# A fence behind the power of the attention output's norm, an earlier split of the FFN's first weights, and pair sums queued behind powers

## The chip, the cores and the metric

One core of one Trainium2 chip runs the whole program in one launch. The metric is the device time of one execution in microseconds. TensorE is called PE here, VectorE DVE, ScalarE ACT, GpSimd POOL; SyncE (SP) issues most loads.

## The reference

A trunk of two layers on 512 tokens of width 1024, all in float32. Layer 0 has multi-head latent attention, layer 1 attention over the frame's own chunk and 8 earlier ones, with a relative bias; both have a SwiGLU FFN of inner width 2816. Every part is wrapped in two norms.

```python
def rms_norm(x, g):
    xf = x.astype(jnp.float32)
    y = xf * lax.rsqrt(jnp.mean(xf * xf, axis=-1, keepdims=True) + EPS)
    return (y * g.astype(jnp.float32)).astype(x.dtype)

def swiglu(h, w_gate, w_up, w_down):
    return (jax.nn.silu(h @ w_gate) * (h @ w_up)) @ w_down

for layer in range(DEPTH):
    h = rms_norm(x, attn_pre_g[layer])
    y = mla_mixer(h, ...) if layer < N_A_LAYERS else chunked_mixer(h, ...)   # both end in o @ w_o
    x = x + rms_norm(y, attn_post_g[layer])
    h = rms_norm(x, ffn_pre_g[layer])
    f = swiglu(h, ffn_w_gate[layer], ffn_w_up[layer], ffn_w_down[layer])
    x = x + rms_norm(f, ffn_post_g[layer])
```

The change lies around `x + rms_norm(y, attn_post_g)` and the FFN's first products, and at the load of the first weights.

## The kernel before

**Layout.** Activations stand with the feature on the partitions: eight tiles of 128 features by 512 tokens. Every float32 product is made of three matmuls of rounded halves, hi by hi, lo by hi and hi by lo (`mm3`, L376 to L378). So each weight tile is split: a cast on ACT gives the high part (`whi`, L144), a subtraction on DVE the low part (`wlo`, L145).

**The feed.** A class `Feed` holds the plan of all weight tiles in the order in which they are used. `load` (L302) issues a load on SP into one of 5 raw buffers, `split` does the two halves into one of 3 hi and lo buffers of 1152 elements, or, with `room="h"`, into 512-wide pieces of another pool. `next` hands a split tile to the products, and `ahead(n)` loads and splits n tiles beyond it. `behind` names instructions behind which a split is to stand.

**Pairs and sums.** A part of the FFN's products is done in pairs with seven products in place of eight (`Pair`). Their weight sums are made by DVE (L183) and by accumulating transfers that POOL issues (`Pair.begin`, L170).

**The attention's output projection and its norm.** `out_proj` does most output tiles for all 512 tokens, and the last groups in two halves of 256 tokens, so that the norm of the first half runs beside the matmuls of the second. `Post.add_half` is that norm: the squares `sq` on ACT (L456), their sum `acc` on DVE (L462), two transposes `tot` on PE (L472), a reduction `ss` on DVE (L475), the power `r` = (mean + eps)^-0.5 on POOL (L480, in `rstd`), and two transposes on PE that spread `r` over the partitions (`bc`, L498). `apply` then multiplies `y` by `bc` (L668), adds x (L670) and makes the halves of the normalised x with which the FFN's products start. Behind the projection come the FFN's first weights: four chunks of `w_gu0`, then those of `w_gu`.

**The order.** The program is written out as it is to run, and a scheduler then orders each engine's instructions by priority: `first(n)` moves a piece n places earlier, and `tc.issue_after(ins)` makes an instruction stand behind another one, which acts only between instructions of the same engine. Each engine runs its row strictly in order.

Of the kernel before, what the change touches and what calls it, by code (L numbers as in the profile page):

```python
# [68 lines left out]
def trunk(ctx: ExitStack, tc: tile.TileContext, a, out):  # L69
# [73 lines left out]
    def split(dst_hi, dst_lo, src):  # L143
        return (nc.scalar.copy(dst_hi, src),  # L144
                V.tensor_tensor(dst_lo, src, dst_hi.bitcast(F32), op=OP.subtract))  # L145

    def split_scaled(dst_hi, dst_lo, src, col):
        return (nc.scalar.activation(dst_hi, src, AF.Copy, scale=col),
                V.scalar_tensor_tensor(dst_lo, src, col, dst_hi.bitcast(F32), op0=OP.mult, op1=OP.subtract))

    class Pair:
# [12 lines left out]
        def begin(self):  # L164

            r, self.made = self.raw, True
            r[0] = r[3] = r[6] = self.tile(2, wide[0], "sum", 2)
            r[4] = self.tile(2, wide[0], "sum2", 2)
            for j, n in ((0, 3), (4, 0)):
                nc.gpsimd.dma_start(r[j], self.src[n], accum_op=OP.add)  # L170

        def load(self, j):

# [89 lines left out]
    class Feed:  # L263


        def __init__(self):
            self.plan, self.raw, self.ready, self.pos, self.room = [], [], [], 0, {}
            self.behind, self.gate = {}, None

        def add(self, src, n, gain=None, room=None):  # L270
            self.plan.append((src, n, gain, room))
# [33 lines left out]
        def split(self, i):  # L305
            while len(self.ready) <= min(i, len(self.plan) - 1):
                j = len(self.ready)
                self.load(j + 2)
                raw, (src, n, gain, room) = self.raw[j], self.plan[j]
                for f in range(j, min(j + 8, len(self.plan))):  # L310
                    if f < j + 5 and isinstance(self.plan[f][0], Pair) or isinstance(self.plan[f][0], Down):
                        self.load(f)
                if isinstance(src, Down):
                    src.sums(*gain)
                    raw = src.at[gain]
                elif isinstance(src, Pair):
                    src.sums(gain)
                    raw = src.raw[gain]
                elif gain is not None and gain.shape[1] > 2:
                    rv = raw[:, :n].rearrange("p (a b) -> p a b", a=gain.shape[1])  # L320
                    with ExitStack() as st:
                        for b in self.behind.get(j, ()):
                            st.enter_context(tc.issue_after(b.ins))
                        V.tensor_tensor(rv, rv, gain, op=OP.mult)
                    gain = None
                if room is None:
                    at_ = 24 if isinstance(src, Pair) else 0
                    pieces = [tuple(wp.tile([P, 1152], F32R, tag=t, name=name_("w" + t), bufs=3)[:, at_:at_ + 1024]
                                    for t in ("hi", "lo"))]
                else:  # L330
                    pieces = self.room[room]()
                w = pieces[0][0].shape[1]
                if isinstance(raw, list):
                    c = 0
                    for t in raw:
                        c_ = slice(c, c + t.shape[1])
                        split(pieces[0][0][:, c_], pieces[0][1][:, c_], t)
                        c += t.shape[1]
                for c in range(0, 0 if isinstance(raw, list) else n, w):
                    m = min(w, n - c)  # L340
                    with ExitStack() as st:
                        for b in self.behind.get(j, ()):
                            st.enter_context(tc.issue_after(b.ins))
                        if gain is None or isinstance(src, Pair):
                            split(pieces[c // w][0][:, :m], pieces[c // w][1][:, :m], raw[:, c:c + m])
                            continue
                        for d in range(0, m, S):
                            split_scaled(pieces[c // w][0][:, d:d + S], pieces[c // w][1][:, d:d + S],
                                         raw[:, c + d:c + d + S], gain[:, (c + d) // S, 0:1])

                def at(c, m, pieces=pieces, w=w):
                    o = c % w
                    return tuple(t[:, o:o + m] for t in pieces[c // w])

                self.ready.append(at)
# [44 lines left out]
    def some(gen, n):  # L400

        last = None
        for _ in range(n):
            last = next(gen, None) or last
        return last
# [32 lines left out]
    class Sum:  # L438
# [28 lines left out]
        def total(self, h=None, ahead=0):  # L467
# [7 lines left out]
                V.reduce_sum(r, t[:, q[0] * P:(q[-1] + 1) * P].rearrange("p (a b) -> p a b", b=P), axis=AX.X)  # L475
            return r

    def rstd(v):
        r = small("r")[:, :v.shape[1]]
        nc.gpsimd.tensor_tensor(r, v, mhalf[:, :v.shape[1]], op=OP.pow)  # L480
        return r

    def rstd_of_scaled(ss, n, r0):
# [125 lines left out]
    class Post:  # L609
# [21 lines left out]
        def add_half(self, h, banks, rest, n1, n2, end=None):  # L631

            with first(40):
                ins = self.half(h, KT - len(banks), banks)
            if end:
                feed.behind[feed.pos] = feed.behind[feed.pos + 1] = ins
            with behind(end):
                at = some(rest, n1)
            with behind(end and at):
                v = self.sum.total(h, 200)  # L640
            with first(200):
                r = rstd(v)
            at = some(rest, n2)
            with behind(end and at):
                self.r[h] = spread(r, 2 * h)
# [37 lines left out]
    def out_proj(rhs, n_k, post, have, n_last, late):  # L683

        done = list(have)

        def weave(gen, each=4):
            ins = None
            for n, ins in enumerate(gen):
                if n % each == each - 1 and done:  # L690
                    post.add(done.pop(0))
            return ins

        groups = GROUPS[n_k][len(have) // 2:]
        for m in groups[:-n_last]:
            b = [bank() for _ in range(m)]
            weave(proj(m, n_k, KC[m], rhs, b))
            done.extend(b)
        last = groups[-n_last:]
        ws = {}  # L700

        def half(h, i, b):
            m, n, end = last[i], 0, i + 1 == n_last
            kc = KC[m]
            chunks = range(-(-n_k // kc))
            for c in chunks[::-1] if h and end else chunks:
                size = min(kc, n_k - c * kc)
                if not h:
                    ws[i, c] = feed.next(size * m * P, not end or c + 1 < len(chunks))
                for kk in range(size):  # L710
                    n += 1
                    for j in range(m):
                        yield mm3(b[j][:, HALF[h]], ws[i, c]((kk * m + j) * P, P), cut(rhs[c * kc + kk], HALF[h]),
                                  n == 1, n == n_k)
                if h and end and c >= len(chunks) - 2:
                    feed.ahead(len(chunks) - 1 - c)

        b = end = None
        for h in range(2):
            k = KT - sum(last)  # L720
            for i, m in enumerate(last):
                first_ = late and not h and not i
                before, b = b, [bank("s"), bank()] if first_ else [bank() for _ in range(m)]
                rest = half(h, i, b)
                if first_:
                    some(rest, 6)
                    for t in late:
                        run(t)
                if h and not i:
                    post.add_half(0, before, rest, 9, 11 if late else 8, end if late else None)  # L730
                elif i:
                    if not h:
                        some(rest, 2)
                    post.half(h, k - last[i - 1], before)
                end = weave(rest, 2 if first_ else 4)
                k += m
        return b

    class Split:
# [36 lines left out]

    def plan_ffn(i):
        for c in range(4):
            feed.add(a["w_gu0"][i, c], 1024, room="h" if c in (1, 2) else None)
        for f in range(N_WHOLE - 2):  # L780
            for c in range(2):
                feed.add(a["w_gu"][i, f, c], 1024)
        feed.add_pairs(a["w_pair"][i])
        feed.add_down(a["w_down"][i])
# [63 lines left out]
    for k in range(KT):  # L848
# [14 lines left out]
                mm3(b1[j], w(j * P, P), xs[k], False, k == KT - 1)  # L863
        if len(x) < KT:
            load_x()
        if k == 3:
            load_positions()
        if k:
            with ExitStack() as order:
# [644 lines left out]
    def products(xs, tb, rb, hid, aside=None):  # L1514
# [7 lines left out]
        for p in range(pairs):  # L1522
# [2 lines left out]
            gate = [U(name="gt") for _ in range(2)]  # L1525
            up_ = [U(name="ut") for _ in range(2)]
            for j in range(7):
                if aside is not None and p and j in (1, 3, 5):
                    next(aside, None)
                w = feed.next(1024, 2)  # L1530
                if p + 1 == pairs and j >= 4:
# [320 lines left out]
```

## Time and profile before

| | us |
|---|---|
| median of the runs | 1108.43 |
| lowest and highest of 3 runs | 1107.37, 1109.54 |
| profiled execution | 1108.42 |
| its span (first to last instruction) | 1106.5 |
| PE busy | 1092.9 |
| DVE busy | 908.8 |
| ACT busy | 679.0 |
| POOL busy | 118.2 |

The granted clock of PE was 0.998 of full speed over the span. The rows of the trace below give a start (us from the start of the span), a length, the engine, the line, the operation with its output and inputs, and in brackets how long the engine stood idle before it and what ended that. A row with x2 joins two instructions. A busy share near 100% says that an engine had work, not that every other engine was late: what PE waits for is read from the waits.

### The profile page before, as it was taken

To read this page: it belongs to the slowest core of one execution; us is meant where nothing else is said; L and a number is where in the kernel's file an instruction comes from. 1 tells how busy PE (TensorE), PEld (TensorE's weight loads), DVE (VectorE), ACT (ScalarE), POOL (GpSimd) and SP (SyncE) were. 2 spreads that over 40 slices of the span, in tenths; PEclk is the share of its full clock that TensorE was granted. 3 is DMA by queue.
4 is the path that set the end of the run, shared out by engine and by line. 5 is a ranking of instruction groups with operands and counts; after the bars stand their busy time and mean duration, and the time that the engine had idled before them with its cause. 6 is when DMAs were issued, how large, how long until landed. Compare 5 with 4: busy or idle time off the path is not lost. (4 is left out here: it accounts for less than half of the span.)

```text
span 1106.5 us, 19053 instructions
## 1 busy us (share of the span) xinstructions
PE 1092.9 (99%) x6893; PEld 978.6 (88%) x6893; DVE 908.8 (82%) x1651; ACT 679.0 (61%) x1319; POOL 118.2 (11%) x181
## 2 busy tenths in 40 slices
PE   9999999999999999999999999999999999999997
PEld 6887889999999998888888888889999999998885
DVE  7787747988878879978867888758988888889977
ACT  7575736755555556668635767656745555556675
POOL 2211100001000001500000110001000010002301
PEclk9999999999999999999999999999999999999999
DMA  7344227427677757961556677636438778859913
GB/s 239 117 118 138 66 69 256 153 76 193 171 205 182 178 171 247 160 193 47 190 146 169 166 193 189 162 115 215 162 92 214 207 198 220 210 177 280 172 29 76
DMA packets 88334, 181.47 MB, mean 164 GB/s; under 512 B 26816, under 2 KB 28608, under 8 KB 88240
## 3 DMA queue, kind: packets, MB, share of 16 engines
q1 hardware_dynamic: 74752, 147.10, 42.8%
q0 software_dynamic: 13056, 32.73, 16.7%
q8 instruction: 54, 0.88, 0.3%
q10 hardware_dynamic: 432, 0.44, 0.1%
q14 instruction: 40, 0.33, 0.1%
HBM read 148.88 MB, written 10.88 MB: 144 GB/s over the span
## 5 line engine op out<-in xcount | busy, mean ns | idle before, releaser
L144 ACT CAST whi<-raw 128x1024 fp32r<-128x1024 f32 (+3 forms) x224 | 225.4, 1006 | 218.2 <-PE al L1544 71.3
L145 DVE TENSOR_TENSOR wlo<-raw,whi 128x1024 fp32r<-128x1024 f32 (+3 forms) x224 | 261.0, 1165 | 62.9 <-ACT whi L144 61.9
L1544 PE MATMUL al<-th,whi 128*128 128x256 f32 x432 | 123.0, 285 | 0.2 <-ACT gt L1554 0.2
L1544 PE MATMUL al<-tl,whi 128*128 128x256 f32 x432 | 121.0, 280 | 0.0
L1544 PE MATMUL al<-th,wlo 128*128 128x256 f32 x432 | 121.0, 280 | 0.0
L376 PE MATMUL b<-xh,whi 128*128 128x512 f32 (+1 forms) x298 | 115.1, 386 | 0.0
L377 PE MATMUL b<-xl,whi 128*128 128x512 f32 (+1 forms) x298 | 109.9, 369 | 0.0
L378 PE MATMUL b<-xh,wlo 128*128 128x512 f32 (+1 forms) x298 | 109.5, 368 | 0.3 <-DVE wlo L145 0.3
L1544 PEld LDWEIGHTS al<-th,whi 128*128 128x128 f32 x432 | 81.3, 188 | 2.6 <-ACT gt L1554 0.4
L1544 PEld LDWEIGHTS al<-tl,whi 128*128 128x128 f32 x432 | 81.3, 188 | 0.0
L1544 PEld LDWEIGHTS al<-th,wlo 128*128 128x128 f32 x432 | 81.3, 188 | 0.0
L545 ACT ACTIVATE p<-p,mn 128x128 f32<-128x128 f32 (+1 forms) x96 | 54.1, 563 | 39.2 <-DVE mn L543 37.4
L145 DVE TENSOR_TENSOR ptl<-pt,pth 128x128 fp32r<-128x128 f32 (+1 forms) x96 | 46.6, 486 | 32.9 <-ACT pth L144 31.3
L145 DVE TENSOR_TENSOR wlo<-wd,whi 128x512 fp32r<-128x512 f32 x86 | 56.3, 685 | 14.6 <-ACT whi L144 14.4
L170 POOL DMA_DIRECT2D raw<-in_w_pair x32 | 28.0, 876 | 367.8 <-DMA raw<-in_w_pair 148.5
L378 PEld LDWEIGHTS b<-xh,wlo 128*128 128x128 f32 x298 | 56.2, 189 | 10.2 <-DVE wlo L145 0.7
L144 ACT CAST whi<-wd 128x512 fp32r<-128x512 f32 x86 | 49.8, 619 | 24.5 <-PE al L1300 10.7
L376 PEld LDWEIGHTS b<-xh,whi 128*128 128x128 f32 x298 | 56.5, 190 | 5.7 <-ACT whi L144 0.2
L377 PEld LDWEIGHTS b<-xl,whi 128*128 128x128 f32 x298 | 56.5, 190 | 5.5
L144 ACT CAST pth<-pt 128x128 fp32r<-128x128 f32 (+1 forms) x96 | 40.3, 422 | 30.3 <-PE pt L558 29.4
L1300 PE MATMUL al<-whi,pl 128*128 128x512 f32 x132 | 51.5, 390 | 0.0
L1300 PE MATMUL al<-whi,ph 128*128 128x512 f32 x132 | 51.4, 389 | 0.0
(319 smaller groups left out, 3301.0 us busy)
## 6 DMA issues: line engine op xcount, KB each, us to landing
raw<-in_w_pair SPq DMA_DIRECT2D x88, 512.0 KB, 4.4
raw<-in_w_pair POOLq DMA_DIRECT2D x32, 512.0 KB, 8.0
wd<-in_w_down SPq DMA_DIRECT2D x54, 256.0 KB, 6.0
raw<-in_w_o SPq DMA_DIRECT2D x16, 512.0 KB, 3.5
raw<-in_w_gu SPq DMA_DIRECT2D x16, 512.0 KB, 4.9
raw<-in_w_down SPq DMA_DIRECT2D x16, 512.0 KB, 4.2
raw<-in_w_qkb SPq DMA_DIRECT2D x16, 512.0 KB, 3.5
wd<-in_w_down POOLq DMA_DIRECT2D x22, 256.0 KB, 5.2
```

The lines of the kernel that those rows point to most:

```text
L144: return (nc.scalar.copy(dst_hi, src), V.tensor_tensor(dst_lo, src, dst_hi.bitcast(F32), op=OP.subtract))
L145: V.tensor_tensor(dst_lo, src, dst_hi.bitcast(F32), op=OP.subtract))
L170: nc.gpsimd.dma_start(r[j], self.src[n], accum_op=OP.add)
L376: nc.tensor.matmul(o, l[0], r[0], start=start, stop=False)
L377: nc.tensor.matmul(o, l[0], r[1], start=False, stop=False)
L378: last_mm[0] = nc.tensor.matmul(o, l[1], r[0], start=False, stop=stop)
L545: nc.scalar.activation(p[:, :n], p[:, :n], AF.Exp, bias=mn[:, :1], scale=-1.0, accum_out=self.sums[:, qt:qt + 1])
L1300: nc.tensor.matmul(to[e], l[c], r[d], start=j < 4 and k == 0 and n == 0, stop=k == NF // 2 - 1 and n == 2, skip_group_check=True)
L1544: nc.tensor.matmul(o, l[c], r[d], start=first_ and n == 0, stop=k == K2 - 1 and n == 2, skip_group_check=True)
```

## The change

Six edits:

1. In `add_half`, behind the power, DVE copies `r` into a small tile `f` (the fence). The next six splits of the feed are ordered behind this copy. This replaces an order that, in layer 1, held two splits behind the sums of the first half (`late`, and so `end`, is set in layer 1 only).
2. At the end of the first half in `out_proj`, `feed.ahead(3)` splits three tiles more, and all four chunks of `w_gu0` go to the 512-wide pieces.
3. The accumulating transfers of `Pair.begin` are ordered behind the last power issued.
4. `Feed.low` holds the last low part; a multiplication of weights by their gains (L324) is ordered behind it on DVE.
5. The positions are loaded at step 6 of the first projection, not at step 3.
6. A side job beside the FFN's pairs (`aside`) also advances at j = 0.

```diff
@@ Pair.begin
             for j, n in ((0, 3), (4, 0)):
-                nc.gpsimd.dma_start(r[j], self.src[n], accum_op=OP.add)
+                with tc.issue_after(last_pow[0].ins):
+                    nc.gpsimd.dma_start(r[j], self.src[n], accum_op=OP.add)
@@ Feed.split
-                        for b in self.behind.get(j, ()):
+                        for b in self.behind.get(j, ()) or (self.low,):
                             st.enter_context(tc.issue_after(b.ins))
                         V.tensor_tensor(rv, rv, gain, op=OP.mult)
...
-                            split(pieces[c // w][0][:, :m], pieces[c // w][1][:, :m], raw[:, c:c + m])
+                            self.low = split(pieces[c // w][0][:, :m], pieces[c // w][1][:, :m], raw[:, c:c + m])[1]
@@ rstd
+    last_pow = [None]
+
     def rstd(v):
         r = small("r")[:, :v.shape[1]]
-        nc.gpsimd.tensor_tensor(r, v, mhalf[:, :v.shape[1]], op=OP.pow)
+        last_pow[0] = nc.gpsimd.tensor_tensor(r, v, mhalf[:, :v.shape[1]], op=OP.pow)
         return r
@@ Post.add_half
             with first(40):
                 ins = self.half(h, KT - len(banks), banks)
-            if end:
-                feed.behind[feed.pos] = feed.behind[feed.pos + 1] = ins
             with behind(end):
                 at = some(rest, n1)
             with behind(end and at):
                 v = self.sum.total(h, 200)
             with first(200):
                 r = rstd(v)
+                fence = V.tensor_copy(small("f")[:, :v.shape[1]], r),
+            for n in range(len(feed.ready), len(feed.ready) + 6):
+                feed.behind[n] = fence
@@ out_proj
                 end = weave(rest, 2 if first_ else 4)
                 k += m
+            if not h:
+                feed.ahead(3)
@@ plan_ffn
         for c in range(4):
-            feed.add(a["w_gu0"][i, c], 1024, room="h" if c in (1, 2) else None)
+            feed.add(a["w_gu0"][i, c], 1024, room="h")
@@ first projection
-        if k == 3:
+        if k == 6:
             load_positions()
@@ FFN pairs
-                if aside is not None and p and j in (1, 3, 5):
+                if aside is not None and p and j in (0, 1, 3, 5):
                     next(aside, None)
```

How this moves instructions shows in each engine's row. In the names the number is a buffer's; `oh`, `ol` are the halves of the attention's output, `wh` those of the weights in 512-wide pieces, `whi` and `wlo` those in wide buffers, `b` a bank of products. All rows are of layer 1, around the end of the projection's first half.

DVE before, from the last sums ahead of the reduction of the first half:

```order
L462 TENSOR_TENSOR acc_1721_8676<-acc_1721_8676,sq_1746_8799 128x256
L462 TENSOR_TENSOR acc_1721_8676<-acc_1721_8676,sq_1747_8802 128x256
L145 TENSOR_TENSOR wlo_1760_8904<-raw_1722_8678,whi_1759_8903 128x1024
L145 TENSOR_TENSOR wlo_1798_9069<-raw_1761_8931,whi_1797_9068 128x1024
L475 TENSOR_REDUCE ss_1751_8839<-tot_1750_8836 128x2
L145 TENSOR_TENSOR wlo_1805_9108<-raw_1788_9025,whi_1804_9107 128x1024
L462 TENSOR_TENSOR acc_1721_8676<-acc_1721_8676,sq_1756_8869 128x256
L668 TENSOR_TENSOR y_1720_8674<-y_1720_8674,bc_1753_8864 128x256
```

DVE now, at the same place:

```order
L145 TENSOR_TENSOR wh_1767_8842<-raw_1755_8819,wh_1766_8841 128x512
L145 TENSOR_TENSOR wh_1769_8844<-raw_1755_8819,wh_1768_8843 128x512
L463 TENSOR_TENSOR acc_1727_8688<-acc_1727_8688,sq_1772_8851 128x256
L463 TENSOR_TENSOR acc_1727_8688<-acc_1727_8688,sq_1773_8854 128x256
L476 TENSOR_REDUCE ss_1777_8891<-tot_1776_8888 128x2
L463 TENSOR_TENSOR acc_1727_8688<-acc_1727_8688,sq_1783_8923 128x256
L644 COPY f_1779_8895<-r_1778_8893 128x2
L463 TENSOR_TENSOR acc_1727_8688<-acc_1727_8688,sq_1784_8926 128x256
L672 TENSOR_TENSOR y_1726_8686<-y_1726_8686,bc_1780_8918 128x256
```

Ahead of the reduction there now stand the sums, and behind it no `wlo` but the fence; eight 512-wide subtractions have come ahead of the sums.

ACT before, from the last group of squares of the first half to the first square of the second:

```order
L456 ACTIVATE sq_1746_8799<-b_1733_8727 128x256
L456 ACTIVATE sq_1747_8802<-b_1734_8728 128x256
L618 ACTIVATE y_1748_8805<-b_1733_8727,gains_70 128x256
L618 ACTIVATE y_1749_8807<-b_1734_8728,gains_70 128x256
L144 CAST whi_1759_8903<-raw_1722_8678 128x1024
L144 CAST whi_1797_9068<-raw_1761_8931 128x1024
L144 CAST whi_1804_9107<-raw_1788_9025 128x1024
L456 ACTIVATE sq_1756_8869<-b_1744_8797 128x256
```

ACT now, up to the same group's squares (`sq_1772`, `sq_1773`):

```order
L144 CAST wh_1751_8811<-raw_1728_8690 128x512
L144 CAST wh_1753_8813<-raw_1728_8690 128x512
L144 CAST wh_1756_8821<-raw_1741_8741 128x512
L144 CAST wh_1758_8823<-raw_1741_8741 128x512
L144 CAST wh_1761_8831<-raw_1750_8809 128x512
L144 CAST wh_1763_8833<-raw_1750_8809 128x512
L144 CAST wh_1766_8841<-raw_1755_8819 128x512
L144 CAST whi_1816_9131<-raw_1760_8829 128x1024
L144 CAST wh_1768_8843<-raw_1755_8819 128x512
L144 CAST whi_1868_9392<-raw_1765_8839 128x1024
L457 ACTIVATE sq_1772_8851<-b_1739_8739 128x256
L457 ACTIVATE sq_1773_8854<-b_1740_8740 128x256
```

Ten casts, two of them of 1024 elements and of chunks behind `w_gu0`, now stand ahead of the squares on which `acc` and `tot` rest.

PE now, from just ahead of `tot` to `bc` (before, 21 matmuls stood between the two, and `tot` stood 23 rows earlier):

```order
L378 MATMUL b_1781_8921<-ol_1600_8161,wh_1742_8743 128x256
L473 MATMUL tot_1776_8888<-ident_87,acc_1727_8688 128x128 x2
L379 MATMUL b_1781_8921<-oh_1599_8160,wh_1743_8744 128x256
L377 MATMUL b_1782_8922<-oh_1599_8160,wh_1742_8743 128x256
L378 MATMUL b_1782_8922<-ol_1600_8161,wh_1742_8743 128x256
L379 MATMUL b_1782_8922<-oh_1599_8160,wh_1743_8744 128x256
L377 MATMUL b_1781_8921<-oh_1649_8343,wh_1742_8743 128x256
L378 MATMUL b_1781_8921<-ol_1650_8344,wh_1742_8743 128x256
L501 MATMUL bc_1780_8918<-ident_87,r_1778_8893 128x128 x2
L379 MATMUL b_1781_8921<-oh_1649_8343,wh_1743_8744 128x256
```

Six matmuls are left between `tot` and `bc`; in layer 0 it is ten.

More of the change, by code (lines that the diff above doesn't have):

```diff
@@ L267, in __init__ @@
             self.plan, self.raw, self.ready, self.pos, self.room = [], [], [], 0, {}
-            self.behind, self.gate = {}, None
+            self.behind, self.gate, self.low = {}, None, None
         def add(self, src, n, gain=None, room=None):
@@ L344, in split @@
                         if gain is None or isinstance(src, Pair):
-                            split(pieces[c // w][0][:, :m], pieces[c // w][1][:, :m], raw[:, c:c + m])
+                            self.low = split(pieces[c // w][0][:, :m], pieces[c // w][1][:, :m], raw[:, c:c + m])[1]
                             continue
                         for d in range(0, m, S):
-                            split_scaled(pieces[c // w][0][:, d:d + S], pieces[c // w][1][:, d:d + S],
-                                         raw[:, c + d:c + d + S], gain[:, (c + d) // S, 0:1])
+                            self.low = split_scaled(pieces[c // w][0][:, d:d + S], pieces[c // w][1][:, d:d + S],
+                                                    raw[:, c + d:c + d + S], gain[:, (c + d) // S, 0:1])[1]
                 def at(c, m, pieces=pieces, w=w):
```

## The prediction, made before the changed kernel was run

> **What bounds the kernel now.** The page's busy table comes first: its columns are busy time, share of the span and instructions of each engine.
>
> ```profile
> PE 1092.9 (99%) x6893; PEld 978.6 (88%) x6893; DVE 908.8 (82%) x1651; ACT 679.0 (61%) x1319; POOL 118.2 (11%) x181
> ```
>
> TensorE (PE) is the bound: 1106.5 us of span less 1092.9 leaves 13.6 us in which it does nothing. None of the edits removes a matmul, so this change can only gain what PE waits for. The table of PE's waits (us in total, times, longest) says what that is:
>
> ```profile
> PE bc L498 <- POOL r L480: 1.9, 2, 1.4
> ...
> PE b L378 <- DVE wlo L145: 0.3, 1, 0.3
> ...
> ```
>
> The first row is the place of the change: twice, once in each layer, the broadcast `bc` of the norm's first half waits for the power on POOL. The last row shown is at the start. The rows left out are places that no edit touches. The timeline of PE around the two places (start, length, instruction, in brackets the idle time):
>
> ```profile
> 180.32 0.38 PE L472 MATMUL tot<-ident,acc 128*128 128x128 f32 x2
> ...
> 182.92 0.28 PE L378 MATMUL b<-oh,wh 128*128 128x256 f32 x1
> 183.79 0.43 PE L498 MATMUL bc<-ident,r 128*128 128x128 f32 x2 [0.58 <-POOL r L480]
> ...
> 756.45 0.38 PE L472 MATMUL tot<-ident,acc 128*128 128x128 f32 x2
> ...
> 759.06 0.28 PE L378 MATMUL b<-oh,wh 128*128 128x256 f32 x1
> 760.69 0.43 PE L498 MATMUL bc<-ident,r 128*128 128x128 f32 x2 [1.36 <-POOL r L480]
> ```
>
> From `tot` to the last matmul before `bc` go 2.60 us (182.92 - 180.32) for 2 transposes and 20 steps, 0.118 us a step. The start of `bc` is 0.87 and 1.63 us after the start before it; less one step that is 0.75 us lost in layer 0 and 1.51 in layer 1. DVE and POOL show why:
>
> ```profile
> 757.37 1.23 DVE L145 TENSOR_TENSOR wlo<-raw,whi 128x1024 fp32r<-128x1024 f32 x1 [0.65 <-ACT whi L144]
> 758.51 0.42 DVE L475 TENSOR_REDUCE ss<-tot 128x2 f32<-128x256 f32 x1
> 758.84 1.21 DVE L145 TENSOR_TENSOR wlo<-raw,whi 128x1024 fp32r<-128x1024 f32 x1
> ...
> 182.21 1.52 POOL L480 TENSOR_TENSOR r<-ss,mhalf 128x2 f32<-128x2 f32 x1 [12.96 <-DVE ss L475]
> 759.08 1.56 POOL L480 TENSOR_TENSOR r<-ss,mhalf 128x2 f32<-128x2 f32 x1 [12.16 <-DVE ss L475]
> 770.97 0.74 POOL L480 TENSOR_TENSOR r<-ss,mhalf 128x2 f32<-128x2 f32 x1 [10.33 <-DVE ss L475]
> ```
>
> `tot` is ready at 756.83, but the reduction starts at 758.51, behind a 1.23-us subtraction `wlo`; then the power takes 1.56 us beside the next `wlo` (758.84 to 760.05), where the same power alone took 0.74. In the second half (770.97) `bc` had 42 matmuls of cover and waits for nothing.
>
> **The fence and the early split.** Both keep `wlo` away from the reduction and the power. What the chain then needs, from the same rows and the second half's reduction:
>
> ```profile
> 770.41 0.42 DVE L475 TENSOR_REDUCE ss<-tot 128x2 f32<-128x256 f32 x1
> ```
>
> `tot` 0.38, a hand-over that I put at 0.1 (POOL to PE takes 0.06 at 183.73), reduction to power 0.56 (770.41 to 770.97), power 0.74, hand-over 0.06: 1.84 us. What covers it is shorter now: the order has 10 matmuls between `tot` and `bc` in layer 0 and 6 in layer 1, where it had 21. With the 2 transposes that is 12 and 8 steps, 1.42 and 0.94 us. So if `acc` is in time, 0.42 us are lost in layer 0 (gain 0.33) and 0.90 in layer 1 (gain 0.61). The wait does not go; it shrinks.
>
> Bounds for layer 0: with the power still at 1.52 the loss is 1.20 (gain -0.45); with no loss left, 0.75. I take 0.35, since the row without a subtraction, 770.97, is the one that the order now resembles: behind the reduction stands only the fence, in layer 1 an `acc` as well. The Trainium skill, "SBUF — State Buffer", in the section on who interferes with whom, says that a DVE operation with two SBUF inputs locks out a GpSimd one that reads SBUF. By that rule layer 1's `acc`, with two such inputs, still holds the power for some 0.3 us, and the sum below would be 0.6, the time 1107.8; this trace agrees on the direction with 1.52 and 1.56 against 0.74.
>
> **What now stands ahead of the squares.** The fence orders DVE alone. ACT's casts of the split are free to run, and the order puts eight half-wide casts of the first FFN weights and one (layer 0) or two (layer 1) 1024-wide casts of later chunks ahead of the last squares on ACT, on which `acc`, `tot`, the power and `bc` hang. The rows that price this:
>
> ```profile
> 174.21 0.90 ACT L618 ACTIVATE y<-b,gains 128x256 f32<-128x256 f32 x2
> ...
> 748.93 1.19 ACT L144 CAST wh<-raw 128x512 fp32r<-128x512 f32 x2
> 749.96 0.72 ACT L456 ACTIVATE sq<-b 128x256 f32<-128x256 f32 x2
> 750.49 0.91 ACT L618 ACTIVATE y<-b,gains 128x256 f32<-128x256 f32 x2
> 753.05 0.74 ACT L456 ACTIVATE sq<-b 128x256 f32<-128x256 f32 x2 [1.65 <-PE b L378]
> 756.29 1.05 ACT L144 CAST whi<-raw 128x1024 fp32r<-128x1024 f32 x1 [0.83 <-DMA raw<-in_w_gu]
> ...
> 753.47 0.96 DVE L462 TENSOR_TENSOR acc<-acc,sq 128x256 f32<-128x256 f32 x2 [1.58 <-ACT sq L456]
> ```
>
> Layer 1: the casts can start at 751.40 (750.49 + 0.91); two take 1.03 to the next start (748.93 to 749.96), so eight end at about 755.5, and two wide ones, 0.95 each (1.05 less the overlap with the next), at 757.4. From squares to the end of `acc` is 1.38 (753.05 to 754.43): 758.8. `tot` stands 23 steps later than before, at 756.45 + 23 x 0.118 = 759.16, so ACT's work alone is in time by 0.35 us. But the last cast also needs its load, the sixth of the gate and up weights, whose buffer comes free only when the first chunk is split: two casts to 752.4 and a subtraction of 512, half of 1.23, so about 753.1. The time of these loads from issue to landing has two rows (count, KB each, median us), around layer 1 and around layer 0, and the transfer that ran beside them one on the page:
>
> ```profile
> raw<-in_w_gu SPq DMA_DIRECT2D x7, 512.0 KB, 4.4
> ...
> raw<-in_w_gu SPq DMA_DIRECT2D x6, 512.0 KB, 7.5
> ...
> raw<-in_w_pair POOLq DMA_DIRECT2D x32, 512.0 KB, 8.0
> ...
> 745.98 0.94 POOL L170 DMA_DIRECT2D raw<-in_w_pair  x1 [39.42 <-DMA raw<-in_w_pair]
> ```
>
> With 4.4 it lands at 757.5; cast 0.95, squares and sums 1.38, so `tot` at 759.85 and `bc` at 761.7, against 759.16 + 0.94 = 760.1 without a wait: 1.6 lost, 0.1 more than before. With 3.7 or less it costs nothing and the gain is 0.61. The accumulating transfer that POOL started at 745.98 is gone from this stretch, which speaks for the shorter time, and 4.4 was measured beside it; I take a gain of 0.25, between -0.1 and 0.61, with -0.3 as the end for 4.6. Layer 0 by the same rows: casts from 175.1, eight to 179.2, one wide one to 180.2, `acc` at 181.5, against `tot` 11 steps later at 181.6: in time.
>
> **The pair sums behind the powers.** Two accumulating transfers a layer now queue on POOL behind the three powers, the last of which is the FFN's:
>
> ```profile
> 795.24 1.07 POOL L480 TENSOR_TENSOR r<-ss,mhalf 128x4 f32<-128x4 f32 x1 [22.67 <-DVE ss L475]
> ...
> 829.62 1.23 DVE L183 TENSOR_TENSOR raw<-raw,raw 128x1024 f32<-128x1024 f32 x1
> ```
>
> So they start at 796.3 instead of 745.98 and 771, and with the page's 8.0 us have landed by 806. The first pair sum that reads such a tile is at 829.62, with its split just ahead: some 20 us of cover. Cost 0; without the cover, 8 us a layer.
>
> **The start.** The positions' loads move behind three loads of `w_aq`:
>
> ```profile
> 15.13 1.35 SPq L837 DMA_DIRECT2D pos_i<-in_positions  x3
> 16.57 1.79 SPq L302 DMA_DIRECT2D raw<-in_w_aq  x4
> ...
> 20.94 0.84 ACT L144 CAST whi<-raw 128x768 fp32r<-128x768 f32 x1 [0.70 <-DMA raw<-in_w_aq]
> ...
> 21.91 0.41 PE L376 MATMUL b<-xh,whi 128*128 128x512 f32 x1
> 22.16 0.40 PE L377 MATMUL b<-xl,whi 128*128 128x512 f32 x1
> 22.82 0.50 PE L378 MATMUL b<-xh,wlo 128*128 128x512 f32 x1 [0.26 <-DVE wlo L145]
> ...
> 24.41 0.22 DVE L894 CAST rot<-pos_i 128x128 f32<-128x128 int32 x1
> ```
>
> `w_aq` is issued 1.4 us sooner. Its cast had waited 0.70 for the load, its `wlo` then held PE back: 0.66 us from start to start, where the step before was 0.25, so 0.41 us. That can go whole, or stay if the loads share the DMA with the others: 0 to 0.41. I take 0.3, since the cast's wait of 0.70 is shorter than the 1.4. The positions are read at 24.41; they now go out by about 18.4 (16.57 + 1.79), 6 us ahead, where `w_aq`, a far larger load, was cast 4.4 us after its first issue. In time: 0.
>
> **The gains behind the low parts, and the earlier side steps.** `low` only orders DVE's multiplications of weights by gains behind the previous split; `aside` advances one place earlier in a stage in which PE waits for nothing. Both have PE's queue of ready work as cover, and cost 0.
>
> **The second half.** The next six splits wait for the second fence too, so three `wlo` stand right behind it and ahead of the normalised x of that half. Each takes 1.2 us; PE has 42 matmuls, 5 us, there. I put 0 to 0.5 us of loss, and take 0.
>
> **The sum.** 0.35 + 0.25 + 0.3 = 0.9 us. The profiled execution took 1108.42 (span 1106.5 and 1.9 around it), the median of the runs is 1108.43, so both give 1107.5. From no change a measurement here can tell about 0.2%, 2.2 us (below 1106.2 or above 1110.6).
>
> **Rivals.** (a) *All three waits vanish.* 0.75 + 1.51 + 0.41 = 2.67, to 1105.7. For it: the reduction and power no longer meet a `wlo`. Against: 6 and 10 matmuls do not cover 1.84 us. A second way to the same time is the clock (two starts, and windows with the busy time of PE, PEld, DVE, ACT and POOL, the granted clock, the DMA share and GB/s):
>
> ```profile
> 104.65 0.48 PE L378 MATMUL b<-ckh,wlo 128*128 128x512 f32 x1
> 107.05 0.49 PE L1088 MATMUL sc<-kh,qh 128*128 128x128 f32 x2 [1.92 <-ACT kh L144]
> ...
> 108.00:111.40 3.40, 3.40 (x15) 3.25 (x14) 2.78 (x8) 1.15 (x5) 0.92 (x2) 0.50 0.98 306
> ...
> 750.00:775.00 25.00, 23.64 (x198) 23.43 (x197) 20.63 (x45) 16.50 (x39) 3.15 (x3) 1.00 0.64 192
> ```
>
> After PE's gap of 2.4 us the granted clock was 0.50 for 3.4 us (108.0 to 111.4), which costs 1.7 us; the gap of 1.5 us at 759 brought none (1.00 from 750 to 775). A start that is shifted by a few tenths may spare it: 1107.5 - 1.7 = 1105.8. The Trainium skill, "TensorE: Matmul & The Clock Gate", says of what happens there that utilisation is judged in free-running windows of 3413 ns and one idle window halves the clock; by that, whether this gap is hit depends on its phase, and the 3.4 us of the row agree with the length.
>
> (b) *ACT's queue holds the norm back; slower.* If the sixth load takes 7.5 us, it lands at 760.6, the squares start at 761.5, `tot` 762.9, `bc` 764.8 against 760.1: 4.7 lost where 1.51 were, 3.2 worse. A gap of that length would also bring the half clock, 1.7. Less 0.65 for the other terms: 4.25, to 1112.7. It decides from about 5.5 us on, where PE's gap (2.7) passes that of 104.65. For it: the 7.5 of layer 0; against: the transfer beside it then is gone.
>
> (c) *Nothing is gained.* `acc` doubles the power again and the second half's splits delay x by 0.5: in the terms' order -0.1, -0.1 and 0.3, less 0.5: 0.4 slower, 1108.8.
>
> **Chances.** The forecast 0.55 (1106.4 to 1108.5), (c) 0.12, (a) 0.19, (b) 0.14. Faster is (a), 0.19; slower is (b), 0.14; the same is the rest, 0.67. The range reaches to (a) at 1105.7, and above to a half clock window met by the forecast or a load a little past its median, 1107.5 + 2.3 = 1109.8; (b) is left out.
>
> **What would show it.** `bc` waits of about 0.4 and 0.7 to 1.7 us in PE's waits; powers of 0.74 to 1.1; no wait of L378 at 22; squares of layer 1 starting near 757.5 to 758.5, idle before them owed to a load; accumulating transfers near 218 and 795. Wrong it is if the squares start after 760, or if another matmul appears among PE's waits.

## The result

In 20 executions of each, the changed kernel took 1107.61 us in the median (1104.39 to 1109.72) and the kernel before 1111.95 (1107.37 to 1117.6). The ratio is 0.9961, with a 95% interval of 0.9947 to 0.9975: 4.3 us faster, of which the interval leaves 2.8 to 5.9. The three times of before that stood ahead of the prediction (1107.37, 1108.43, 1109.54) are the first of its 20 and lie among the fastest seven; the changed kernel's median is about as fast as the fastest of before, and none of its executions goes beyond 1110.

The two profiled executions show nothing of this gain: 1108.42 with a span of 1106.5 before, 1109.37 with a span of 1107.4 after. The busy table after:

```profile
PE 1094.4 (99%) x6893; PEld 979.9 (88%) x6893; DVE 909.3 (82%) x1659; ACT 680.5 (61%) x1323; POOL 117.1 (11%) x181
```

PE's waits after (us in total, times, longest):

```profile
PE sc L1094 <- ACT kh L144: 1.9, 1, 1.9
PE warm L113 <- DVE idle L110: 1.2, 1, 1.2
PE bc L501 <- POOL r L483: 0.9, 2, 0.7
PE b L377 <- ACT y L621: 0.8, 1, 0.8
PE al L1550 <- ACT gt L1560: 0.2, 1, 0.2
PE b L379 <- DVE wlo L145: 0.2, 1, 0.2
```

The wait of `bc` fell from 1.9 to 0.9 and did not go, and a matmul of layer 1 that had not waited now waits 0.8 for a bank. The timeline of layer 1 after, first ACT, then DVE, POOL and PE:

```profile
750.77 3.83 ACT L144 CAST wh<-raw 128x512 fp32r<-128x512 f32 x7
755.46 1.05 ACT L144 CAST whi<-raw 128x1024 fp32r<-128x1024 f32 x1 [0.86 <-DMA raw<-in_w_gu]
...
757.49 1.05 ACT L144 CAST whi<-raw 128x1024 fp32r<-128x1024 f32 x1 [0.46 <-DMA raw<-in_w_gu]
758.45 0.65 ACT L457 ACTIVATE sq<-b 128x256 f32<-128x256 f32 x2
758.99 0.84 ACT L621 ACTIVATE y<-b,gains 128x256 f32<-128x256 f32 x2
...
760.34 0.42 DVE L476 TENSOR_REDUCE ss<-tot 128x2 f32<-128x256 f32 x1 [0.53 <-PE tot L473]
760.68 0.42 DVE L463 TENSOR_TENSOR acc<-acc,sq 128x256 f32<-128x256 f32 x1
...
760.92 0.77 POOL L483 TENSOR_TENSOR r<-ss,mhalf 128x2 f32<-128x2 f32 x1 [54.04 <-DVE ss L476]
...
759.51 0.38 PE L377 MATMUL b<-oh,wh 128*128 128x256 f32 x1 [0.84 <-ACT y L621]
...
759.87 0.44 PE L473 MATMUL tot<-ident,acc 128*128 128x128 f32 x2
761.74 0.43 PE L501 MATMUL bc<-ident,r 128*128 128x128 f32 x2 [0.72 <-POOL r L483]
```

The reduction now follows `tot` at once, and the power takes 0.77 where it took 1.56. But ACT stands twice at casts for loads (0.86 and 0.46) before it comes to the squares at 758.45, and so `tot` starts at 759.87. The copy `y` (L621) behind the squares frees a bank, which is the new wait.

So the question is where 4.3 us come from, if one execution of each shows none of it.

### The profile page after: what moved, and what is told of

Read it like the earlier page. It is cut to its first block, busy times and chain, and to the rows that moved or that the text cites. A ratio compares the mean times of both kernels' runs of the same rounds, so it can differ in the third digit from the quotient of the medians.

```text
span 1107.4 us, 19059 instructions
## 1 busy us (share of the span) xinstructions
PE 1094.4 (99%) x6893; PEld 979.9 (88%) x6893; DVE 909.3 (82%) x1659; ACT 680.5 (61%) x1323; POOL 117.1 (11%) x181
## 5 line engine op out<-in xcount | busy, mean ns | idle before, releaser
L144 ACT CAST whi<-raw 128x1024 fp32r<-128x1024 f32 (+3 forms) x220 | 221.7, 1008 | 208.7 <-PE al L1550 69.4
L145 DVE TENSOR_TENSOR wlo<-raw,whi 128x1024 fp32r<-128x1024 f32 (+3 forms) x220 | 256.5, 1167 | 69.4 <-ACT whi L144 68.3
L377 PE MATMUL b<-xh,whi 128*128 128x512 f32 x234 | 96.7, 414 | 0.0
L379 PE MATMUL b<-xh,wlo 128*128 128x512 f32 x234 | 91.9, 393 | 0.2 <-DVE wlo L145 0.2
L378 PE MATMUL b<-xl,whi 128*128 128x512 f32 x234 | 91.7, 392 | 0.0
L379 PEld LDWEIGHTS b<-xh,wlo 128*128 128x128 f32 x234 | 43.9, 188 | 10.5 <-DVE wlo L145 0.9
L1306 PE MATMUL al<-wlo,ph 128*128 128x512 f32 x132 | 51.3, 389 | 0.0
L184 DVE TENSOR_TENSOR raw<-raw,raw 128x1024 f32<-128x1024 f32 x40 | 48.9, 1223 | 0.5
```

The lines of the kernel that those rows point to most:

```text
L144: return (nc.scalar.copy(dst_hi, src), V.tensor_tensor(dst_lo, src, dst_hi.bitcast(F32), op=OP.subtract))
L184: V.tensor_tensor(t, x, y, op=OP.add)
L377: nc.tensor.matmul(o, l[0], r[0], start=start, stop=False)
L378: nc.tensor.matmul(o, l[0], r[1], start=False, stop=False)
L379: last_mm[0] = nc.tensor.matmul(o, l[1], r[0], start=False, stop=stop)
L1306: nc.tensor.matmul(to[e], l[c], r[d], start=j < 4 and k == 0 and n == 0, stop=k == NF // 2 - 1 and n == 2, skip_group_check=True)
```

## The experiments

Each kernel was timed in turn with the kernel before on the same chip, in three batches; ratios are against before. The microseconds gained or lost in the text are the ratio's share of before's time; the differences of the medians (before: 1110.61 beside e1 to e4, 1111.35 beside e5 to e8, 1110.79 beside e9 to e12) lie up to about 1 us from them. "Sums" is edit 3, "low" edit 4, "positions" edit 5, "aside" edit 6, as they are numbered in the change.

| kernel | median us | ratio, 95% interval | executions |
|---|---|---|---|
| before, unchanged (e1) | 1110.68 | 1.0009 [0.9993, 1.0024] | 12 |
| before + sums (e2) | 1108.08 | 0.9968 [0.9955, 0.9982] | 12 |
| before + fence + early split (e3) | 1114.60 | 1.0032 [1.0017, 1.0046] | 11 |
| before + low + positions + aside (e4) | 1107.79 | 0.9969 [0.9956, 0.9981] | 11 |
| before + low (e5) | 1109.27 | 0.9981 [0.9969, 0.9992] | 12 |
| before + aside (e6) | 1109.82 | 0.9991 [0.9978, 1.0004] | 12 |
| before + positions (e7) | 1109.70 | 0.9988 [0.9974, 1.0002] | 12 |
| changed, without fence and early split (e8) | 1105.09 | 0.9951 [0.9932, 0.9970] | 6 |
| changed (e9) | 1107.31 | 0.9965 [0.9951, 0.9979] | 12 |
| changed, without early split (e10) | 1104.81 | 0.9943 [0.9926, 0.9960] | 6 |
| changed, without fence (e11) | 1107.16 | 0.9963 [0.9950, 0.9976] | 8 |
| e8 again (e12) | 1104.71 | 0.9941 [0.9925, 0.9957] | 6 |

**e1, the kernel before once more.** No edit.

> The kernel before, unchanged, for a second trace of it. Theory A (late loads: in most executions of before the reduction on DVE stands behind subtractions whose loads land late, so bc waits longer than in the execution that was shown): ratio 1.00, and if its profiled execution takes over 1110 us, the waits of bc on the power sum to over 3 us instead of 1.9. Theory B (half clock: the gaps are as long as shown, but more of the free windows fall into them): the same waits, and a mean granted clock of 0.995 or less. Theory C (the start: the loads of w_aq behind the positions are late): the time is lost before 40 us.

Its profiled execution took 1109.52, 1.1 us more than the one shown, and its table of waits has rows that the first one lacks:

```profile
PE bc L498 <- POOL r L480: 2.3, 2, 1.7
...
PE al L1544 <- DVE ut L1556: 0.9, 1, 0.9
PE b L1701 <- ACT pth L144: 0.8, 1, 0.8
PE b L1701 <- DVE ptl L145: 0.4, 1, 0.4
```

None of the three theories named these. Nor does theory B, the half clock, explain the gain: the mean granted clock of this execution is 0.999, and over all executions of the batches it averages 0.9974 in the changed kernel's 20 and 0.9973, 0.9969 and 0.9970 in the 35, 29 and 19 of before. Of a span of 1106 us the largest of these differences, 0.0005, is about 0.6 us (an estimate), against 4.3.

`al` waits in the FFN's pairs of layer 1, `L1701` in the attention of layer 1, both far from the norm. DVE in the second place, with the matmul that waited:

```profile
606.70 1.23 DVE L324 TENSOR_TENSOR raw<-raw,gains 128x1024 f32<-128x1024 f32 x1 [1.22 <-DMA raw<-in_w_qkb]
609.38 1.23 DVE L324 TENSOR_TENSOR raw<-raw,gains 128x1024 f32<-128x1024 f32 x1 [0.55 <-DMA raw<-in_w_qkb]
...
609.98 0.85 PE L1701 MATMUL b<-pth,vb 128*128 128x512 f32 x4 [0.77 <-ACT pth L144]
```

DVE stands idle at multiplications of weights by gains whose loads have not landed, and the softmax's work behind them is late: behind the first of these rows comes the scores' step on DVE (L543), for which ACT waits 2.60 us at 608.86, then `pth`, then PE. The same line in the trace that was shown ahead of the prediction, in the view of this line:

```profile
L324 DVE TENSOR_TENSOR raw<-raw,gains x16: 1164/1220/1226, 538.7 to 645.0; 128x1024 f32<-128x1024 f32 x16
...
  DMA raw<-in_w_qkb: 7.3, 5
```

DVE was idle for 7.3 us there in five waits, and PE happened not to be reached by it. In e1 it is 9.0 us in seven. From this came theories D and E of the next batch.

**e2, the sums alone.** The edit (the lines that set `last_pow` are left out):

```diff
-                nc.gpsimd.dma_start(r[j], self.src[n], accum_op=OP.add)
+                with tc.issue_after(last_pow[0].ins):
+                    nc.gpsimd.dma_start(r[j], self.src[n], accum_op=OP.add)
```

> Before with the accumulating transfers ordered behind the last power, nothing else. Theory A, in the form that these transfers make the loads late: 2 to 4 us faster, with waits of bc under 1 us each. Theory A, in the form that the order of DVE and ACT makes it: 0 to 1 us. Theories B and C: no change (under 1 us).

Ratio 0.9968, 3.5 us faster, with waits of `bc` under 1 us, as theory A said in the form that the transfers make the loads late. Its trace, ACT, DVE and PE at the first half's norm in layer 1:

```profile
755.74 2.95 ACT L144 CAST whi<-raw 128x1024 fp32r<-128x1024 f32 x3
...
756.82 2.36 DVE L145 TENSOR_TENSOR wlo<-raw,whi 128x1024 fp32r<-128x1024 f32 x2 [1.07 <-ACT whi L144]
759.10 0.42 DVE L476 TENSOR_REDUCE ss<-tot 128x2 f32<-128x256 f32 x1
...
757.78 0.38 PE L473 MATMUL tot<-ident,acc 128*128 128x128 f32 x2
761.29 0.43 PE L501 MATMUL bc<-ident,r 128*128 128x128 f32 x2 [0.62 <-POOL r L483]
```

Before, the second of these casts waited 0.83 for its load; now three run on end, the two subtractions too, and the reduction starts 1.32 us after `tot` where it took 2.06. The waits of `bc` sum to 0.6 (none in layer 0), against 1.9 and 2.3 in the two traces of before and 2.4 to 3.0 in those of e4 to e7. These 1.3 to 2.4 us are seen; the rest of the 3.5, whose interval goes down to 2.0, was not traced to a place. The profiled execution itself took 1109.60, since in it PE waits another 2.7 us in the attention of layer 1, at the place of e1.

That the loads are the link shows in all traces: in the six without the edit and without the early split (before, e1, e4 to e7) ACT waits 0.8 to 1.5 us in each layer at a cast whose load is late; in the four with the edit and without the early split (e2, e8, e10, e12) it waits for no such load. The time from issue to landing (median of the loads in the window), layer 0 and layer 1 in e2:

```profile
raw<-in_w_gu SPq DMA_DIRECT2D x6, 512.0 KB, 5.8
...
raw<-in_w_gu SPq DMA_DIRECT2D x7, 512.0 KB, 4.6
```

In layer 0 it fell from 7.5; in layer 1 the median did not fall (4.4 before), only the wait at the cast went. How the transfers delay the loads is not shown.

**e3, the fence and the early split alone.** Edits 1 and 2.

> Before with the fence and the early split of the first FFN weights, nothing else; the accumulating transfers stay where they were. Theory A by the order: 3 to 4 us faster. Theory A by the transfers: under 1.5 us faster, and ACT's squares of layer 1 wait for a load. Theory B: 1 to 2 us faster, with fewer half windows. Theory C: no change.

Ratio 1.0032: 3.5 us slower. No theory had expected a loss. PE's waits, and ACT ahead of the squares in layer 1:

```profile
PE b L376 <- ACT y L618: 2.1, 1, 2.1
...
PE tot L472 <- DVE acc L462: 1.3, 1, 1.3
```

```profile
756.10 1.14 ACT L144 CAST wh<-raw 128x512 fp32r<-128x512 f32 x2 [1.62 <-DMA raw<-in_w_gu]
757.45 0.62 ACT L144 CAST wh<-raw 128x512 fp32r<-128x512 f32 x1 [0.21 <-DMA raw<-in_w_gu]
758.74 1.05 ACT L144 CAST whi<-raw 128x1024 fp32r<-128x1024 f32 x1 [0.66 <-DMA raw<-in_w_gu]
...
761.16 0.65 ACT L456 ACTIVATE sq<-b 128x256 f32<-128x256 f32 x2
```

With the accumulating transfers still beside the loads, ACT waits 2.5 us for them in three places, against 1.3 in the changed kernel, and comes to the squares at 761.16, 2.7 later than there; 1.4 of these it was behind already ahead of the casts (the copies `y` start at 751.50 and 750.06). The loads take 5.8 us in layer 1 and 6.5 in layer 0, against 4.8 and 5.1 in the changed kernel, which at this place differs in the transfers. In layer 0 `tot` waits 1.3 for `acc`, in layer 1 a matmul 2.1 for a bank. This is the mechanism of the prediction's rival (b), in a kernel where the transfers were not moved away. About 1.2 us of the loss may be the clock (an estimate: 0.9962 over its 11 executions against 0.9973, of a span of 1106).

**e4, the three other edits.** Low, positions and aside.

> Before with the three other edits: the positions loaded three steps later, the gains behind the low parts, the side job at j = 0. Theories A and B: within 0.5 us of before (0.3 from the start, as predicted). Theory C: 3 to 4 us faster, gained before 40 us.

Ratio 0.9969, 3.4 us, where theories A and B expected at most 0.5. Its table of waits is short, while `bc` waits as before:

```profile
PE bc L498 <- POOL r L480: 2.8, 2, 1.9
...
PE sc L1693 <- DMA k<-f: 0.4, 1, 0.4
```

**e5, e6 and e7 split these three** (of e5 the lines that set `self.low` are left out).

```diff
 e5: -  for b in self.behind.get(j, ()):
     +  for b in self.behind.get(j, ()) or (self.low,):
 e6: -  if aside is not None and p and j in (1, 3, 5):
     +  if aside is not None and p and j in (0, 1, 3, 5):
 e7: -  if k == 3:
     +  if k == 6:
```

> Before with the gains' multiplications ordered behind the previous low part, nothing else. Theory D (DVE, whose row is strict, stands at multiplications whose loads have not landed, and the attention's ptl queue behind them; the load is later in some executions than in the one shown): about 2 us faster, of the 3.4 that the three edits gave together, no multiplication of L325 idle on a load, no wait of L1701 on ptl or pth. Rival E (it is the side job's transposes, whose x lands late): no change. Rival C (the start): no change.

> Before with the side job advancing at j = 0 as well, nothing else. Rival E: 1 to 3 us faster, and no wait of al on ut near 960 to 1000; the multiplications wait for loads as before. Theory D: within 0.5 us, the stalls of 0.4 to 1.7 us near 619 to 630 stay.

> Before with the positions loaded three steps later, nothing else. The prediction put 0.3 us on it. Theories D and E: 0 to 0.4 us faster, the wait of L378 at the start gone. Rival C: 2 to 3 us faster.

Low brought 2.1 us, with an interval clear of no change, as theory D said. Its multiplications (still L324 in this kernel) now run until 674.1 instead of 645.0, and the view of the line, whose list of idle times was headed by 7.3 and 9.0 us, has none:

```profile
L324 DVE TENSOR_TENSOR raw<-raw,gains x16: 1172/1220/1223, 540.4 to 674.1; 128x1024 f32<-128x1024 f32 x16
its engine sat idle before it (us, times) until:
...
```

The other traces agree. In the six without low DVE stands idle at these multiplications for 7.3 to 11.3 us, and in five of them PE waits in this attention, 1.0 to 2.7 us in all; in the eight with low there is neither.

Aside brought 1.0 and positions 1.3, both with an interval that just includes no change; together the three sum to 4.4, against 3.4 for e4, which their intervals allow. So neither the start nor the side job alone is the cause. Whether each has a part the times leave open; the traces show one for each. That of aside, in the view of its transposes, before (e1) and with the edit (e6):

```profile
L1216 DVE STREAM_TRANSPOSE xt<-x x8: 697/706/712, 842.5 to 987.7; 128x512 f32<-128x512 f32 x8
...
  DMA x<-mid: 3.7, 4
```

```profile
L1216 DVE STREAM_TRANSPOSE xt<-x x8: 705/711/717, 846.0 to 946.7; 128x512 f32<-128x512 f32 x8
...
  DMA x<-mid: 1.1, 1
```

DVE stood 3.7 us at transposes whose x was still loading, the last at 987.7, and `ut` behind them was late for PE's `al`: 0.9 in e1. Done by 946.7, they wait once. Over all traces DVE waits 2.7 to 5.4 us for these loads in the six without aside and at most 1.7 in the eight with it; `al` waits for `ut` (0.3 to 0.9) in three of the six and in none of the eight. The start in e5, which lacks the edit on the positions:

```profile
23.17 0.50 PE L376 MATMUL b<-xh,whi 128*128 128x512 f32 x1 [0.58 <-ACT whi L144]
24.16 0.50 PE L378 MATMUL b<-xh,wlo 128*128 128x512 f32 x1 [0.26 <-DVE wlo L145]
```

Two waits there, 0.58 and 0.26, where the trace shown had only the second; with the edit alone (e7) one of 0.15 is left. PE waits 0.3 to 0.8 us there in the six traces without the edit and at most 0.2 in the eight with it. e6's trace, which lacks low, shows what a stall in the attention can cost beyond the wait; in the second row the number ahead of the last two is the granted clock:

```profile
612.97 1.24 PE L1701 MATMUL b<-pth,vb 128*128 128x512 f32 x4 [1.81 <-ACT pth L144]
...
613.00:617.00 4.00, 4.00 (x14) 3.49 (x15) 3.57 (x8) 2.96 (x6) 1.24 (x3) 0.57 0.24 65
```

At 0.57 over 4 us, up to 1.7 us come on top of the 1.81.

**e8, and then the four kernels of the last batch.** All hold sums, low, positions and aside; they differ in the fence and the early split.

> The changed kernel without the fence and the early split: the sums behind the powers and the three other edits. If the parts add up (sums -3.5, others -3.4, fence and early split +3.5): 6 to 7 us faster than before, so faster than the changed kernel's 4.3. If the loss of the fence and the early split came only from the accumulating transfers that ran beside them, and the sums already hold the gain: 4 to 5 us, level with the changed kernel. If the fence brings its own gain once the sums are moved: 2 to 4 us.

> The changed kernel again, as the mark for the three beside it, which all hold the sums behind the powers and the three other edits. About 4.3 us faster than before (ratio 0.996); waits of bc of 0.2 and 0.7 us, and a matmul of layer 1 that waits 0.8 us for a bank.

> The changed kernel without the early split: the fence stays. Theory F (the early split costs, since its casts stand ahead of ACT's squares and copies; the fence helps or is neutral): 5 to 6 us faster than before, level with the kernel that has neither. Rival G (the fence costs, since three subtractions stand behind it and the FFN's first x late): 4 us faster or less, and a wait of the FFN's first products on wlo.

> The changed kernel without the fence: the early split stays. Theory F: 3 to 4.5 us faster than before, with the wait of L377 for ACT's y in layer 1 as in the changed kernel. Rival G: 5 to 6 us faster.

> The kernel without the fence and the early split, a second time, since its first measurement rests on few executions. If that holds: 5 to 6 us faster than before, 1 to 2 us faster than the changed kernel. If the first was luck: 4.3 us, level with the changed kernel.

Theory F holds, with a little more than its 5 to 6 us for e10 and e12 (6.3 and 6.6), and no trace shows the wait on `wlo` that rival G expected. Without the early split the kernels take 1104.81 (with the fence) and 1104.71 (without), each between 1103.27 and 1105.86 in six executions; with it 1107.31 and 1107.16. The early split costs 2.4 to 2.6 us, the fence nothing that shows. Sums and others gave 3.5 and 3.4 alone, and 5.4 [3.3, 7.6] and 6.6 [4.8, 8.3] together in the two measurements, so whether they add up to 6.9 stays open. In the trace the fence does what it is for (e10, DVE, POOL and PE at layer 1):

```profile
754.91 0.42 DVE L476 TENSOR_REDUCE ss<-tot 128x2 f32<-128x256 f32 x1 [2.45 <-PE tot L473]
756.24 0.17 DVE L644 COPY f<-r 128x2 f32<-128x2 f32 x1 [0.91 <-POOL r L483]
...
755.49 0.72 POOL L483 TENSOR_TENSOR r<-ss,mhalf 128x2 f32<-128x2 f32 x1 [51.33 <-DVE ss L476]
...
757.22 0.38 PE L501 MATMUL bc<-ident,r 128*128 128x128 f32 x2
```

The power takes 0.72 and `bc` waits for nothing, where e12, without the fence, waits 0.6 in layer 1. That 0.6 is too little to be seen in the times. What the early split costs is seen for the greater part. In e9 `bc` waits 0.9 and the bank 0.7, 1.6 in all, against 0 in e10; in e11, against the 0.6 of e12, it is 2.5:

```profile
PE bc L501 <- POOL r L483: 1.6, 1, 1.6
...
PE b L377 <- ACT y L621: 0.9, 1, 0.9
```

The clock does not separate these two, with a mean of 0.9972 in both.

## Why the prediction came out as it did

*The time.* 1107.5 was forecast and 1107.61 measured, but the change was forecast as one that could not be told from none, and it is 4.3 us faster. That the number agrees is luck: the prediction took before's time from three executions at the low end of its spread, and from the median of all 20, 1111.95, the same gain of 0.9 would have led to 1111.05. It judged the changed kernel's waits about rightly and the spread of before not at all.

*The fence and the early split.* The working for layer 1 was close: squares at 758.45 (757.5 to 758.5 forecast), `tot` at 759.87 (759.85 for a landing of 4.4), `bc` at 761.74 (761.7). The loss of 1.6 us forecast for that case came in two parts, 0.7 at `bc` and 0.8 at the bank. The second was named only as a sign of error. In the waits layer 1 so lost 0.2 (1.56 against 1.36), where a gain of 0.25 was taken from the range; layer 0 gained 0.36, where 0.35 was taken. Layer 0 came out at 0.22 in the waits, 0.38 in starts, against 0.42. A power without a `wlo` beside it takes 0.77 (after) and 0.72 (e10), with one 1.56 (before). The rule of the Trainium skill's "SBUF — State Buffer" (who interferes with whom) agrees with these; the 0.3 us that it was taken to add for layer 1's `acc` did not come, since the `acc` overlapped the power for 0.2 us only (760.68 + 0.42 against 760.92). In the second half, where 0 was taken, PE waits for nothing.

*What the two parts are worth.* The prediction gave them 0.6 us together. Alone (e3) they cost 3.5, and with the sums moved the early split costs 2.5 and the fence 0. Rival (b), ACT's queue, is the mechanism of the part of that loss that the waits show; it was right in kind, and with the sums moved it is smaller.

*The sums: cost 0, no gain.* The cost came out as said; that no gain was put on it is the first failing term. The prediction saw that the transfer at 745.98 would leave the stretch, and used it only to shorten one landing in layer 1. But the transfers also held back the loads on which the kernel before waited at the norm: with the sums alone (e2) `bc` of layer 0 waits for nothing, and in layer 1 for 0.62 in place of 1.36, although the reduction still stands behind a `wlo` and the power still takes 1.56. Measured alone, this edit gave 3.5.

*"Cost 0, with PE's queue of ready work as cover" for low and aside.* The second failing step. The cover was read from one execution in which PE waited for none of it. The order shows that low moves 16 multiplications far back in DVE's row, and the trace had DVE idle for 7.3 us at them, waiting for loads; that was not read as a stall that other executions pass on to PE. Low alone gave 2.1 and aside 1.0 (an interval that includes 0); with the positions the three gave 3.4.

*The start.* 0.3 forecast, 1.3 [-0.2, 2.9] measured alone. Both a cast and a subtraction can be late there, as e5 shows. In the changed kernel one wait of 0.2 remains (L379), so that step's sign, that the wait goes, did not come.

*The half clock.* By rival (a) it might have gone at 108. It stayed in the profiled execution after (0.996 over the span).

## What to carry to other kernels

An instruction that stands in a strict row at a load that has not landed can be a cost even where the profiled execution shows no one waiting for it: look for idle time owed to a DMA on every engine, not only on the bound one, and move such work behind what others need. Before a gain is claimed for a piece of a bundled change, run the pieces: here the first two that the title names were worth 0 and -2.5 us, and a moved pair of transfers and three small edits made the gain. The versions without the early split take 1104.7 to 1104.8 us, less than both kernels.

## What was not expected of the hardware

The same gap of PE, 2.18 us lost near 105 (2.40 from start to start, less a step), halved the granted clock for a while in nine of the 14 traces (0.91 over the 20 us, in before 0.50 for 3.4 us) and left it at 1.00 in five, e1 among them:

```profile
100.00:120.00 20.00, 17.99 (x101) 14.91 (x101) 16.81 (x43) 15.29 (x37) 3.46 (x6) 1.00 0.39 109
```

Of ten other gaps of 1.5 to 2.25 us two did so, those of e3 in layer 1 and of e6 in the attention. The Trainium skill, "TensorE: Matmul & The Clock Gate", in the section on what is actually happening, says that the activity window is free-running, so that where in it work falls shifts the change of the clock. That the same gap is hit in nine traces and spared in five agrees with this. The same section of the Trainium skill has the cold clock come after an idle window of about 3.4 us; here gaps of about 2.0 to 2.25 us were enough. One execution can therefore differ from the next by 1.7 us (3.4 us at half the clock) with no wait that differs.
